# A mixture-of-experts layer whose residual rows come from the expert gathers in place of gathers of their own

## The chip, the cores and the metric

One core of a Trainium2 chip runs the kernel. The metric is device microseconds of one execution; the kernel before takes 515.84 us (median of 3 runs, 515.18 to 518.26). One further execution was profiled, and every row below is of that one.

## The reference

One encoder layer on 512 tokens of 1024 features, all in float32: a mixing half (differential attention and a bidirectional recurrence), then a mixture of experts with a residual, then a final norm. The change lies in the second half.

```python
    h = rmsnorm(x, norm2_g[l])
    x = x + hierarchical_moe(h, w_grp[l], w_exp[l], w_gate[l], w_up[l], w_down[l])
return rmsnorm(x, final_g)
...
def hierarchical_moe(h, w_grp, w_exp, w_gate, w_up, w_down):
    g_prob = jax.nn.softmax((t @ w_grp).astype(jnp.float32), axis=-1)
    g_top_p, g_idx = lax.top_k(g_prob, 1)
...
    e_top_logit, e_idx = lax.top_k(e_in_grp, TOP_K)
    e_w = jax.nn.softmax(e_top_logit, axis=-1) * g_top_p
    global_idx = g_idx * EXPERTS_PER_GROUP + e_idx
...
    for e in range(N_EXPERTS):
        hid = jax.nn.silu(t @ w_gate[e]) * (t @ w_up[e])
        out = out + comb[:, e:e + 1] * (hid @ w_down[e])
```

There are 4 groups of 8 experts with a hidden width of 256. A token chooses one group and in it two experts, so both experts of a token are in the same group.

## The kernel before

**Order of the work.** Nothing is issued in the order of the source. Each piece of work is a `task` with an engine, a cost, what it reads and writes, and a priority (`pri`, lower first). `Plan.run` (L188) plays all tasks through a model of the engines and so fixes the order of every engine's queue; the numbers that set priorities stand in one table, `PRM` (L349). Where the plan sees PE idle it puts in small matmuls on zeros (L531, fillers), so that PE stays active. A DMA has a planned time to landing (`lat`; 4.0 for a gather, L1112).

**Mixing half, up to some 245 us.** It leaves x, the residual stream, in SBUF as four tiles of 128 tokens. The output projection of the attention adds its results to x on DVE (L851) or, after a pass on ACT, on POOL (L849); the bits of `ap` in the table say which.

**Router.** `tok_pair(u)` (L883) handles tiles 2u and 2u+1. SP writes x to a DRAM copy, `x2d`. PE transposes x (L897) and multiplies by the router's weights (L906: a moving slice of 128 columns, of which 36 count, 32 experts and 4 groups). DVE picks the group and the two experts (`f1`, L924 to L939). A matmul with a triangle of ones ranks the tokens of each expert (L947, L948); `f3` (L958, L959) takes each token's rank. `hot` (L964) makes one-hots E of the rank among an expert's 64 slots, and L984 makes those among 256 places in a group (EG). `f4`, `f5` (L994 to L1005) compute the two weights of a token. POOL multiplies the choice with what is to travel to the slots: the token's number, its place in its group (L976), its weight and its norm factor (L1009), in a tile `ohw` with three columns of 32.

`tables()` (L1013) turns these round with matmuls by the one-hots (`spread`, L1021): `idx`, the token of each slot (bank `b`, four DVE operations L1030 and L1033), and `slot`, three values a slot (bank `b3`, copied by `g7`, L1039): column 0 is the place, 1 the weight, 2 the norm factor. `places` (L1049) gives `gidx`, the token at each place of a group (DVE, L1053 to L1055).

**Experts.** 16 pairs n of experts, two at a time, 64 slots each, so a pair fills 128 partitions. `gather(n)` (L1122): POOL fetches the rows of x of a pair by `idx` from `x2d` (L1114, an indirect DMA of up to 128 x 4 KB) into one of three buffers XG, in turn, so pairs n and n+3 share one; PE transposes them (L1133, 8 matmuls), DVE and ACT copy them out with the norm's gain (L1137, L1143). The three buffers are zeroed once by POOL (L1125). `expert_pair(n)` (L1146): gate and up matmuls (L1154, 32 records in the trace), silu (L1159, ACT) times up (L1161, DVE), two transposes (L1167) and their copy (L1170, ACT), a one-hot `pm` of the places (L1173, DVE), down matmuls (L1181, two halves of 512 columns). The result, scaled by the weight, is split in two float32r parts: ACT writes `yh` (L482), DVE the rest `yl` (L483).

**Residual and sum.** `places_of(g)` (L1192), once for each group of 4 pairs: POOL zeroes two accumulators of 128 places (L1195) and gathers the group's rows of x into them by `gidx`. `combine(n)` (L1199) multiplies `pm` with `yh` and `yl` (L1214), and DVE adds the result to the accumulators (L1217). After a group's fourth pair `final` (L1222) computes the norm (squares L1230 and L1231, the power on POOL L1235, scaling L1237) and POOL scatters the rows to the output (L1243). In the last pair the second half's accumulator is taken into the bank by PE (L1209).

**Weights.** SP issues 6 MB of weights a pair (L1097 gate and up, L1104 down, L1109 the last pair's down) as soon as buffers are free.

Of the kernel before, what the change touches and what calls it, by code (L numbers as in the profile page):

```python
# [117 lines left out]
class Plan:  # L118
# [69 lines left out]
    def run(self):  # L188
# [85 lines left out]
        while left:  # L274
# [81 lines left out]
def kernel(ctx: ExitStack, tc: tile.TileContext, a, info=None):  # L356
# [42 lines left out]
    slot, idx, g2T, wr = fixed(3 * NP), fixed(NP, I32), fixed(KD), fixed(KD * 36 + 92)  # L399
# [425 lines left out]
    def out_unit(ks, t, n):  # L825
# [3 lines left out]
        for g in sorted({k // 2 for k in ks}):  # L829
# [28 lines left out]
    oht, ohw, gtok = buf(NT * 2 * NE, F32R), buf(NT * 6 * NE), buf(NT * NG, F32R)  # L858
# [3 lines left out]
    slotv = slot.t.rearrange("p (a n) -> p a n", a=3)  # L862

    def load_router(pri):
# [18 lines left out]
    def tok_pair(u):  # L883
# [558 lines left out]
```

## Time and profile before

| | |
|---|---|
| runs of before | 515.18, 515.84, 518.26 us |
| profiled execution | 518.9 us; span 517.1 us, mean granted clock 0.988 |
| PE busy | 495.7 us (96% of the span), 3178 matmul records |
| DVE, ACT, POOL busy | 296.9 (57%), 210.2 (41%), 198.2 us (38%) |
| moved by DMA | 130.56 MB |
| queue of POOL's DMAs | 8.40 MB |
| first transposes of the experts (L1133) start | 267.40 us |
| last down matmul (L1181) ends | 504.7 us |
| gathers (L1114) | 24: 16 for pairs, 8 for accumulators |

The profile's times are us from the start of the span. A "bank" is a PSUM bank, `big` and `sml` are SBUF buffers, `fix` a tile that stays. A record's duration on PE holds some overlap with its neighbours, so sums over PE's work are taken from the chain, which counts each stretch once. Idle time of an engine names who released it.

### The profile page before, as it was taken

What the parts mean: (1) busy time and instruction counts of PE and PEld (TensorE: products, weight loads), DVE (VectorE), ACT (ScalarE), POOL (GpSimd) and SP (SyncE); (2) the same over time, 40 slices, a digit from 0 to 9 for tenths busy, and PEclk for the clock granted to TensorE, in tenths of its full rate; (3) what the DMA queues carried; (4) which work ended last, traced back from release to release, by engine and by line L of the source; (5) the groups of instructions that cost most, each with busy time, mean ns of one, the idle gap of its engine ahead of it and who ended that gap; (6) DMA issues with size and microseconds to landing.
All of it is one profiled execution on the core that took longest, in us unless ns stands there. A gap on an engine that the chain in (4) does not pass through costs nothing.

```text
span 517.1 us, 8524 instructions
## 1 busy us (share of the span) xinstructions
PE 495.7 (96%) x3178; PEld 339.0 (66%) x3178; DVE 296.9 (57%) x551; ACT 210.2 (41%) x424; POOL 198.2 (38%) x264
## 2 busy tenths in 40 slices
PE   9898999999999999999889999999999989999992
PEld 9897789978999878888873344444445434444441
DVE  2887665988868699695750243446433642641324
ACT  4563688768345546346113222242222322321112
POOL 4789825685687721227453030006100430210002
PEclk9899999999999999999999999999999989999997
DMA  8583000310252650989967999999999999999930
GB/s 300 141 292 108 1 1 1 117 46 1 82 176 83 176 150 21 357 317 363 371 199 246 372 412 411 409 413 380 381 408 415 412 410 389 343 412 416 405 122 36
DMA packets 47941, 130.56 MB, mean 252 GB/s; under 512 B 10861, under 2 KB 21274, under 8 KB 44058
## 3 DMA queue, kind: packets, MB, share of 16 engines
q1 hardware_dynamic: 43002, 120.91, 62.2%
q0 software_dynamic: 4608, 8.40, 4.7%
q10 hardware_dynamic: 288, 0.69, 0.5%
q8 instruction: 26, 0.43, 0.3%
q14 instruction: 17, 0.14, 0.1%
HBM read 132.07 MB, written 6.29 MB: 268 GB/s over the span
## 4 chain that ended last, share of the span: by engine, by line
PE 69%; POOL 8%; issue 8%; DMA 8%; DVE 4%; ACT 2%; SPq 0%; POOLq 0%; ACTq 0%
PE bank L1154 18%; PE bank L606 15%; PE bank L1181 8%; PE bank L838 7%; PE bank L1214 5%; POOL big L472 3%; PE bank L750 2%; DMA big<-x2d,fix 2%; PE bank L531 2%; PE bank L784 2%; PE bank L1133 2%; DMA big<-in_x_dram 2%; DMA big<-in_w_gate_dram 2%; DMA out_dram<-big,fix 1%; PE bank L772 1%
## 5 line engine op out<-in xcount | busy, mean ns | idle before, releaser
L606 PE MATMUL bank<-big,big 128*128 128x256 f32 (+1 forms) x768 | 119.5, 315 | 1.8 <-DVE big L479 1.8
L1154 PE MATMUL bank<-big,big 128*64 128x512 f32 x512 | 117.2, 596 | 0.0
L606 PEld LDWEIGHTS bank<-big,big 128*128 128x128 f32 x768 | 107.4, 193 | 10.6 <-DVE big L479 2.0
L1154 PEld LDWEIGHTS bank<-big,big 128*64 128x64 f32 x512 | 36.2, 137 | 65.1 <-issue 63.2
L483 DVE SCALAR_TENSOR_TENSOR big<-bank,fix,big 128x512 fp32r<-128x512 f32 (+1 forms) x40 | 27.8, 695 | 73.6 <-ACT big L482 70.2
L1217 DVE TENSOR_TENSOR big<-big,bank 128x512 f32<-128x512 f32 x62 | 39.5, 681 | 50.5 <-PE bank L1214 44.1
L1181 PE MATMUL bank<-big,big 128*64 128x512 f32 x256 | 60.0, 608 | 0.0
L1235 POOL TENSOR_TENSOR sml<-sml,fix 128x1 f32<-128x1 f32 x8 | 4.5, 561 | 139.2 <-DVE sml L1234 139.1
L472 POOL TENSOR_TENSOR big<-big,big 128x1024 fp32r<-128x1024 f32 (+2 forms) x21 | 50.4, 2403 | 15.2 <-ACT big L470 8.1
L482 ACT ACTIVATE big<-bank,fix 128x512 fp32r<-128x512 f32 (+1 forms) x40 | 25.7, 644 | 58.5 <-PE bank L1181 51.8
L838 PE MATMUL bank<-big,big 128*128 128x512 f32 x192 | 47.4, 397 | 0.0
L531 PE MATMUL bank<-fix 128*128 128x128 bf16 x617 | 42.5, 228 | 1.7 <-DVE fix L533 1.0
L531 PEld LDWEIGHTS <-fix 128*128 128x128 bf16 x617 | 38.3, 102 | 8.1 <-issue 7.0
L1181 PEld LDWEIGHTS bank<-big,big 128*64 128x64 f32 x256 | 18.7, 140 | 34.3 <-issue 31.8
L1114 POOL DMA_INDIRECT big<-x2d,fix x24 | 24.8, 1033 | 40.8 <-PE bank L1133 34.3
L838 PEld LDWEIGHTS bank<-big,big 128*128 128x128 f32 x192 | 35.1, 188 | 8.2 <-issue 1.1
L1159 ACT ACTIVATE big<-bank,fix 128x256 f32<-128x256 f32 x16 | 7.6, 474 | 76.8 <-PE bank L1154 72.3
L472 DVE TENSOR_TENSOR big<-big,big 128x1024 fp32r<-128x1024 f32 (+1 forms) x16 | 30.4, 1912 | 10.2 <-PE bank L606 4.7
L1214 PE MATMUL bank<-big,big 128*128 128x512 f32 x128 | 35.4, 411 | 0.0
L470 ACT CAST big<-big 128x1024 fp32r<-128x1024 f32 (+2 forms) x27 | 27.1, 1016 | 16.6 <-PE bank L606 4.9
L1214 PEld LDWEIGHTS bank<-big,big 128*128 128x128 f32 x128 | 22.4, 189 | 15.0 <-issue 11.4
L479 DVE TENSOR_TENSOR big<-bank,big 128x512 fp32r<-128x512 f32 (+1 forms) x40 | 24.3, 629 | 8.1 <-ACT big L478 8.0
(194 smaller groups left out, 680.9 us busy)
## 6 DMA issues: line engine op xcount, KB each, us to landing
big<-in_w_down_dram SPq DMA_DIRECT2D x30, 1024.0 KB
big<-in_w_gate_dram SPq DMA_DIRECT2D x60, 512.0 KB
big<-in_w_up_dram SPq DMA_DIRECT2D x60, 512.0 KB
big<-in_w_in_dram SPq DMA_DIRECT2D x20, 512.0 KB
big<-in_w_out_dram SPq DMA_DIRECT2D x4, 1024.0 KB
big<-in_x_dram SPq DMA_DIRECT2D x4, 512.0 KB
big<-in_w_gate_dram SPq DMA_DIRECT2D x8, 256.0 KB
big<-in_w_up_dram SPq DMA_DIRECT2D x8, 256.0 KB
```

Of the source, the lines that this page charges most:

```text
L470: lambda e: (e.copy if e is nc.scalar else e.tensor_copy)(hi(), src()), r=r, w=[kw[0]], pri=pri, room=room, two=True)
L472: lambda e: e.tensor_tensor(lo(), src(), hi().bitcast(F32), op=OP.subtract), r=r + [kw[0]], w=[kw[1]], pri=pri,
L482: task("ACT", act(n), lambda e: e.activation(hi(), src(), AF.Copy, scale=scale), r=[bnk, *r], w=[w[0]], pri=pri)
L483: task("DVE", dve(n) + 0.06, lambda e: e.scalar_tensor_tensor(lo(), src(), scale, hi().bitcast(F32), op0=OP.mult, op1=OP.subtract), r=[bnk ...
L531: e.matmul(b[:, :P], wz.t, wz.t, start=True, stop=True)
L606: e.matmul(out(b), lhs(x, k), rhs(y, k), start=(k == 0 and j == 0), stop=(k == KD - 1 and j == 2))
L838: e.matmul(b.t, lh[x], w[y], start=(i == 0), stop=(i == last))
L1114: g = task("POOL", 1.1, lambda e: e.indirect_dma_start(out=dst.ap(), out_offset=None, in_=x2d[:, :], in_offset=bass.IndirectOffsetOnAxis(a ...
L1154: e.matmul(bg.t[s * 64:(s + 1) * 64].rearrange("p (j f) -> p j f", j=2), xgT[n].ap(KD, P)[:, k, s * 64:(s + 1) * 64], w, start=(k == 0), s ...
L1181: e.matmul(by.t[s * 64:(s + 1) * 64], hidT[n].ap(2, P)[:, k, s * 64:(s + 1) * 64], EW[2 * n + s][1].ap(2, D)[:, k, m * 512:(m + 1) * 512], ...
L1214: e.matmul(b.t, pm.ap()[:, t * P:(t + 1) * P], y.ap(), start=(i == 0 and not held), stop=(i == 1))
L1217: task("DVE", dve(S), lambda e, b=b, xs=xs: e.tensor_tensor(xs(), xs(), b.t, op=OP.add), r=[b], w=[(z, m)])
```

## The change

1. The accumulators are no longer zeroed and filled by gathers. The first pair of a group copies its combined result into them (ACT or DVE, new line L1216); the other three add as before.
2. The residual is added where the expert's result is: a fourth column of the slot table holds 1 where the expert is a token's first and 0 where it is the second. Per half: ACT z = by * slot 1 (new L1185), DVE z += gathered x * slot 3 (new L1186), ACT yh = z (new L1188), DVE yl = z - yh (new L1189).
3. `ohw` and the slot table have four columns, with a copy (new L979) and a memset on POOL.
4. Router logits: 64 columns in place of 128. One-hots: one tensor_tensor for a pair of tiles in place of four tensor_scalar (new L965). Index: token numbers start at -2S and 2S is added, so an empty slot is out of bounds without a test: two operations in place of four. `places` is planned later.
5. Table: `re`, `re3` (what room the loads of weights must leave), `ap` (14 of the additions to x on POOL and 18 on DVE, before 10 and 22), `sq`, `a2`, `o1`, `ot`, `ws`, `w0`; the XG buffers are zeroed earlier.

```diff
+LW = 64
...
-PRM = dict(rw=11000, ro=3000, re=3000, re2=6000, pad=0.4, seq="Q0 X0 X1 K0 V0 G0 G1 V1 Q1 K1", mo=7, mr=7, ge=-42, lru=57,
+PRM = dict(rw=11000, ro=3000, re=0, re2=6000, pad=0.4, seq="Q0 X0 X1 K0 V0 G0 G1 V1 Q1 K1", mo=7, mr=7, ge=-42, lru=57,
...
-                        e.matmul(lgv()[:, t % 2], xT.ap()[:, k * P:(k + 1) * P], wr.t[:, k * 36:k * 36 + P], start=(k == 0), stop=(k == KD - 1))
+                        e.matmul(lgv()[:, t % 2], xT.ap()[:, k * P:(k + 1) * P], wr.t[:, k * 36:k * 36 + LW], start=(k == 0), stop=(k == KD - 1))
...
-        def hot(e, j):
-            for t in range(2):
-                e.tensor_scalar(E.ap(2, 2, P)[:, t, j].rearrange("p (s c) -> p s c", s=2), iot.t[:, None, 0:64].to_broadcast([P, 2, 64]),
-                                rselv[:, 2 * u + t, j:j + 1], None, op0=OP.is_equal)
...
+        def hot(e):
+            e.tensor_tensor(E.ap(4, 2, 64), iot.t[:, None, None, 0:64].to_broadcast([P, 4, 2, 64]),
+                            rselv[:, two].rearrange("p t j -> p (t j)")[:, :, None, None].to_broadcast([P, 4, 2, 64]), op=OP.is_equal)
...
+        task("POOL", 0.3, lambda e: e.tensor_copy(ohw.ap(NT, 2, 4 * NE)[:, two, 0, 3 * NE:], ohp[:, :, 0].bitcast(F32)),
+             r=[(oh, u)], w=[(ohw, (u, 3))])
...
-                e.tensor_scalar(none.ap()[rows], mine, 0.0, 8192.0, op0=OP.is_equal, op1=OP.mult)
-            for s in range(2):
-                rows, mine = slice(s * 64, s * 64 + 64), b.t[s * 64:s * 64 + 64, s:NE:2]
-                e.scalar_tensor_tensor(idx.t[rows], mine, -1.0, none.ap()[rows], op0=OP.add, op1=OP.add)
+                e.tensor_scalar(idx.t[rows], mine, 2.0 * S, None, op0=OP.add)
...
-        task("PE", 1.0, places, r=[*EGs, gtok], w=[bp], pri=pl.pri + 60)
+        task("PE", 1.0, places, r=[*EGs, gtok], w=[bp], pri=pl.pri + 140)
...
-            task("POOL", 1.0, lambda e: e.memset(xg[n].ap(), 0.0), w=[xg[n]], pri=PRM["xz"], after=[mark["lg"]])
+            task("POOL", 1.0, lambda e: e.memset(xg[n].ap(), 0.0), w=[xg[n]], pri=PRM["xz"], after=[mark["o", 2, 1]])
...
-            yh, yl = ys[n][0][m]
-            evac(by, lambda by=by: by.t, lambda yh=yh: yh.ap(), lambda yl=yl: yl.ap(), S, [yh, yl],
-                 scale=slotv[:, 1, n:n + 1], r=[(slot, 1)])
+            (yh, yl), z, xs = ys[n][0][m], buf(S), lambda m=m: xg[n].ap()[:, m * 512:(m + 1) * 512]
+            task("ACT", act(S), lambda e, by=by, z=z: e.activation(z.ap(), by.t, AF.Copy, scale=slotv[:, 1, n:n + 1]), r=[by, (slot, 1)], w=[z])
+            task("DVE", dve(S) + 0.06, lambda e, z=z, xs=xs: e.scalar_tensor_tensor(
+                z.ap(), xs(), slotv[:, 3, n:n + 1], z.ap(), op0=OP.mult, op1=OP.add), r=[xg[n], (slot, 1)], w=[z], two=True)
+            task("ACT", act(S, 0), lambda e, z=z, yh=yh: e.copy(yh.ap(), z.ap()), r=[z], w=[yh])
+            task("DVE", dve(S), lambda e, z=z, yh=yh, yl=yl: e.tensor_tensor(yl.ap(), z.ap(), yh.ap().bitcast(F32), op=OP.subtract),
+                 r=[z, yh], w=[yl], two=True)
...
-    def places_of(g):
-        acc[g] = [buf(D) for _ in range(2)]
-        for q in range(2):
-            task("POOL", 1.0, lambda e, q=q: e.memset(acc[g][q].ap(), 0.0), w=[acc[g][q]],
-                 after=[mark["g", 4 * g - 1] if g else mark["q", 1]])
-            rows_in(acc[g][q], pl.view(gidx, gidx.t[:, q * NG + g:q * NG + g + 1]))
...
+        if n % 4 == 0:
+            acc[n // 4] = [buf(D) for _ in range(2)]
...
-                if not held:
+                if n % 4 == 0:
+                    task({"ACT": act(S, 0), "DVE": dve(S)}, lambda e, b=b, xs=xs: (e.copy if e is nc.scalar else e.tensor_copy)(xs(), b.t),
+                         r=[b], w=[(z, m)])
+                elif not held:
...
-        if n % 4 == 0:
-            pl.pri -= 20
-            places_of(n // 4)
-            pl.pri += 20
```

How it moves instructions is shown at three places. Line numbers in rows of the kernel before are its own, those in rows of the changed kernel are new ones: L1012 is the weights' product (before L1009), L977 the places' (L976), L1213 the combine matmul (L1214), L1237 the power (L1235), L1245 the row scatter (L1243), L532 a filler; L1114, L1133, L1154, L1167 and L1181 are the same in both.

First, POOL at the end of the router, before: the last products into `ohw` and the first three gathers (big_3009, 3036 and 3060 are the XG buffers).

```order
L1009 TENSOR_TENSOR big_2973<-fix 128x4x32 [waits Pool_49]
L976 TENSOR_TENSOR big_2973<-fix,sml_3069 128x4x32 [waits DVE_49]
L1009 TENSOR_TENSOR big_2973<-fix 128x4x32 [waits DVE_49]
L1114 DMA big_3009<-x2d,fix 128x1024 [waits DVE_49,Pool_49]
L1114 DMA big_3036<-x2d,fix 128x1024 [waits Pool_49]
L1114 DMA big_3060<-x2d,fix 128x1024 [waits Pool_49]
```

The same place in the changed kernel, where the XG buffers are big_2751, 2761 and 2773:

```order
L1012 TENSOR_TENSOR big_2151<-fix 128x4x32 [waits Pool_49]
L1012 TENSOR_TENSOR big_2151<-fix 128x4x32 [waits DVE_49]
L977 TENSOR_TENSOR big_2151<-fix,sml_3010 128x4x32 [waits DVE_49,Activation_49]
L1114 DMA big_2751<-x2d,fix 128x1024 [waits DMAHW5_49,DMAHW3_49,DMAHW7_49,DMAHW2_49,DVE_49]
L1114 DMA big_2761<-x2d,fix 128x1024
L1114 DMA big_2773<-x2d,fix 128x1024
L1012 TENSOR_TENSOR big_2151<-fix 128x4x32 [waits DVE_49]
```

The second pair's weight product stood ahead of the first gather and now stands behind the third. The next gather into big_2751 (pair 3) now waits for DVE besides PE.

Second, POOL at the end of group 2, before, with pair 15's gather (into big_3009); big_4317 and 4323 are accumulators of group 3.

```order
L1114 DMA big_4317<-x2d,fix 128x1024 [waits DMASW1_49,Pool_49]
L1114 DMA big_4323<-x2d,fix 128x1024 [waits DMASW2_49,Pool_49]
L1235 TENSOR_TENSOR sml_4427<-sml_4427,fix 128x1 [waits DVE_49]
L1114 DMA big_3009<-x2d,fix 128x1024 [waits DMASW4_49]
L1235 TENSOR_TENSOR sml_4431<-sml_4431,fix 128x1 [waits DVE_49]
L1243 DMA out_dram<-big_4463,fix 512x1024 [waits DVE_49]
```

And in the changed kernel, with pair 15's gather into big_2751:

```order
L1237 TENSOR_TENSOR sml_4469<-sml_4469,fix 128x1 [waits DVE_49,Pool_49]
L1237 TENSOR_TENSOR sml_4471<-sml_4471,fix 128x1 [waits DVE_49,Pool_49]
L1245 DMA out_dram<-big_4485,fix 512x1024 [waits DMAHW6_49,DMAHW4_49,DMAHW7_49,DVE_49,Activation_49]
L1114 DMA big_2751<-x2d,fix 128x1024 [waits DMASW0_49,DVE_49,PE_49]
L1245 DMA out_dram<-big_4516,fix 512x1024 [waits DVE_49,Activation_49]
```

The accumulators' gathers are gone. Pair 15's gather stood ahead of both row scatters of group 2, and now stands behind the first of them and waits for DVE and PE.

Third, PE around pair 15's transposes (L1133), before; the L1181 rows are the last ones of pair 12.

```order
L1181 MATMUL bank_66<-big_4429,big_4480 64x512
L1181 MATMUL bank_66<-big_4439,big_4480 64x512
L1133 MATMUL bank_67<-fix,big_3009 128x128 x4
L1133 MATMUL bank_64<-fix,big_3009 128x128 x4
L1214 MATMUL bank_63<-big_4510,big_4476 128x512
L1214 MATMUL bank_63<-big_4511,big_4476 128x512
L1214 MATMUL bank_62<-big_4510,big_4476 128x512
L1214 MATMUL bank_62<-big_4511,big_4476 128x512
L1154 MATMUL bank_69<-big_4467,big_4243 64x512
```

In the changed kernel the eight L1181 rows of pair 12 stand further up, and between them and these transposes are 16 rows of L1154 and 6 of L1213, of which the last stand here:

```order
L1154 MATMUL bank_69<-big_4480,big_4336 64x512
L1154 MATMUL bank_69<-big_4450,big_4336 64x512
L1154 MATMUL bank_69<-big_4480,big_4336 64x512
L1213 MATMUL bank_67<-big_4497,big_4412 128x512
L1213 MATMUL bank_67<-big_4509,big_4412 128x512
L1213 MATMUL bank_66<-big_4511,big_4412 128x512
L1213 MATMUL bank_66<-big_4521,big_4412 128x512
L1133 MATMUL bank_65<-fix,big_2751 128x128 x4
L1133 MATMUL bank_68<-fix,big_2751 128x128 x4
L1167 MATMUL bank_64<-fix,big_4489 128x128 x2
L1213 MATMUL bank_63<-big_4511,big_4412 128x512
L1213 MATMUL bank_63<-big_4521,big_4412 128x512
```

The transposes of pair 15 followed pair 12's down matmuls directly and now come 22 rows later.

## Rows read from the trace of the kernel before

**Rows 1.** Windows: length; PE, PEld, DVE, ACT, POOL busy (instructions); clock, DMA share, GB/s

```profile
300.00:320.00 20.00, 20.00 (x102) 9.74 (x100) 9.29 (x17) 5.16 (x14) 5.53 (x6) 1.00 1.02 411
420.00:425.00 5.00, 5.00 (x17) 1.58 (x18) 1.36 (x2) 0.69 (x1) 0.85 (x1) 0.68 1.03 413
480.00:500.00 20.00, 20.00 (x111) 8.70 (x108) 6.40 (x12) 2.69 (x5) 0.00 (x0) 1.00 0.79 307
```

**Rows 2.** Waits of SP's queue, 300 to 490 us: total, times, longest

```profile
SPq L1097 <- PE bank L1154: 28.4, 11, 4.8
```

**Rows 3.** The chain that ended last: start, duration, what, times

```profile
290.11 1.09 PE bank L1133 x8
...
307.26 3.43 PE bank L1181 x16
310.69 5.15 PE bank L1154 x24
315.85 2.05 PE bank L1214 x8
...
468.46 1.28 PE bank L531 x21
```

**Rows 4.** PE's timeline, the waits: start, duration, work, [idle before, releaser]

```profile
269.80 1.16 PE L1133 MATMUL bank<-fix,big 128*128 128x128 f32 x8 [1.24 <-DMA big<-x2d,fix]
...
419.29 0.84 PE L1133 MATMUL bank<-fix,big 128*128 128x128 f32 x4 [2.58 <-DMA big<-x2d,fix]
420.06 5.17 PE L1181 MATMUL bank<-big,big 128*64 128x512 f32 x16
```

**Rows 5.** PE's groups by line, 267.4 to 504.8 us: count, busy, mean ns

```profile
L531 PE MATMUL bank<-fix 128*128 128x128 bf16 x159 | 10.9, 220 | 0.0
```

**Rows 6.** PE's timeline in the router

```profile
251.82 1.16 PE L906 MATMUL bank<-fix,big 128*128 128x128 f32 x8
...
261.77 1.14 PE L1049 MATMUL bank<-sml,big 128*128 128x4 f32 x8
```

**Rows 7.** DVE's timeline at the second pair's one-hots and the index

```profile
259.91 1.04 DVE L964 TENSOR_SCALAR big<-fix 128x128 fp32r<-128x128 f32 x4
...
262.05 0.37 DVE L1030 TENSOR_SCALAR sml<-bank 64x16 f32<-64x16 f32 x2
262.45 0.37 DVE L1033 SCALAR_TENSOR_TENSOR fix<-bank,sml 64x16 int32<-64x16 f32 x2
```

**Rows 8.** The page's groups by line: busy us, mean ns

```profile
L1217 DVE TENSOR_TENSOR big<-big,bank 128x512 f32<-128x512 f32 x62 | 39.5, 681 | 50.5 <-PE bank L1214 44.1
```

**Rows 9.** POOL's timeline: the last product, gathers, a scatter, pair 13's gather

```profile
261.95 0.44 POOL L1009 TENSOR_TENSOR big<-fix 128x128 f32<-128x128 f32 x1 [1.48 <-DVE fix L1005]
263.73 1.31 POOL L1114 DMA_INDIRECT big<-x2d,fix  x1 [1.34 <-DVE fix L1055]
...
266.67 0.99 POOL L1114 DMA_INDIRECT big<-x2d,fix  x1 [0.30 <-issue]
...
408.15 1.44 POOL L1243 DMA_INDIRECT out_dram<-big,fix  x1 [2.62 <-issue]
...
411.19 1.04 POOL L1114 DMA_INDIRECT big<-x2d,fix  x1 [0.30 <-DMA big<-in_w_down_dram]
```

**Rows 10.** Landing of gathers issued at 265, at 449, at 412 to 425

```profile
DMA to landing us min/median/max: 4.4/4.4/4.4
...
DMA to landing us min/median/max: 8.2/8.2/8.2
...
DMA to landing us min/median/max: 8.4/9.1/9.7
```

**Rows 11.** ACT's and DVE's timeline at the end

```profile
504.86 0.69 ACT L482 ACTIVATE big<-bank,fix 128x512 fp32r<-128x512 f32 x1 [1.03 <-PE bank L1181]
...
508.35 0.59 ACT L1230 ACTIVATE big<-bank 128x512 f32<-128x512 f32 x1
...
505.58 0.75 DVE L483 SCALAR_TENSOR_TENSOR big<-bank,fix,big 128x512 fp32r<-128x512 f32 x1 [0.97 <-ACT big L482]
```

More of the change, by code (lines that the diff above doesn't have):

```diff
@@ L398 @@
     tokid, desc4, tri, ones = fixed(NT), fixed(NG), fixed(P, BF), fixed(P, BF)
-    slot, idx, g2T, wr = fixed(3 * NP), fixed(NP, I32), fixed(KD), fixed(KD * 36 + 92)
+    slot, idx, g2T, wr = fixed(4 * NP), fixed(NP, I32), fixed(KD), fixed(KD * 36 + LW - 36)
     flag, ovj, nov, novb = fixed(1, I32), fixed(3 * NT), fixed(1), fixed(1, BF)
@@ L861 @@
     w12v, rselv = (z.t.rearrange("p (t j) -> p t j", j=2) for z in (w12, rsel))
-    slotv = slot.t.rearrange("p (a n) -> p a n", a=3)
+    slotv = slot.t.rearrange("p (a n) -> p a n", a=4)
     def load_router(pri):
@@ L879, in load_router @@
         task("POOL", 3.0, g, r=[cst], w=[iot, tokid, desc4, ones, tri], pri=pri, after=[mark[2]])
+        task("POOL", 0.4, lambda e: e.memset(ohw.ap(NT, 2, 4 * NE)[:, :, 1, 3 * NE:], 0.0), w=[(ohw, (0, 3)), (ohw, (1, 3))], pri=pri + 30, after=[mark[9]])
     Es, EGs = [], []
@@ L960, in tok_pair @@
         task("DVE", 0.45, f3, r=[(oh, u), rk], w=[rko, (rsel, u)])
-        def hot(e, j):
-            for t in range(2):
-                e.tensor_scalar(E.ap(2, 2, P)[:, t, j].rearrange("p (s c) -> p s c", s=2), iot.t[:, None, 0:64].to_broadcast([P, 2, 64]),
-                                rselv[:, 2 * u + t, j:j + 1], None, op0=OP.is_equal)
-        ends = [task("DVE", 0.42, lambda e, j=j: hot(e, j), r=[(rsel, u), iot], w=[(E, j)]) for j in range(2)]
+        def hot(e):
+            e.tensor_tensor(E.ap(4, 2, 64), iot.t[:, None, None, 0:64].to_broadcast([P, 4, 2, 64]),
+                            rselv[:, two].rearrange("p t j -> p (t j)")[:, :, None, None].to_broadcast([P, 4, 2, 64]), op=OP.is_equal)
+        ends = [task("DVE", 0.68, hot, r=[(rsel, u), iot], w=[E], two=True)]
         pl.pri += 10
@@ L1013, in tables @@
     def tables():
-        b, b3, bp, none, nog, big = bank(), bank(), bank(), buf(NP), buf(2 * NG), buf(1)
+        b, b3, bp, nog, big = bank(), bank(), bank(), buf(2 * NG), buf(1)
         def spread(e, u, dst, val, f32):
@@ L1029, in g @@
                 rows, mine = slice(s * 64, s * 64 + 64), b.t[s * 64:s * 64 + 64, s:NE:2]
-                e.tensor_scalar(none.ap()[rows], mine, 0.0, 8192.0, op0=OP.is_equal, op1=OP.mult)
-            for s in range(2):
-                rows, mine = slice(s * 64, s * 64 + 64), b.t[s * 64:s * 64 + 64, s:NE:2]
-                e.scalar_tensor_tensor(idx.t[rows], mine, -1.0, none.ap()[rows], op0=OP.add, op1=OP.add)
-        task("DVE", 0.5, g, r=[b], w=[idx, none])
+                e.tensor_scalar(idx.t[rows], mine, 2.0 * S, None, op0=OP.add)
+        task("DVE", 0.37, g, r=[b], w=[idx])
         for u in range(2):
-            task("PE", 0.9, lambda e, u=u: spread(e, u, b3.t[:, :3 * NE], lambda t, j: ohw.ap(NT, 2, 3 * NE)[:, t, j], True),
-                 r=[Es[u], *((ohw, (u, z)) for z in range(3))], w=[b3], pri=pl.pri + 20)
+            task("PE", 0.9, lambda e, u=u: spread(e, u, b3.t[:, :4 * NE], lambda t, j: ohw.ap(NT, 2, 4 * NE)[:, t, j], True),
+                 r=[Es[u], *((ohw, (u, z)) for z in range(4))], w=[b3], pri=pl.pri + 20)
         def g7(e):
@@ L1041, in g7 @@
                 rows = slice(s * 64, s * 64 + 64)
-                e.tensor_copy(slotv[rows], b3.t[rows, :3 * NE].rearrange("p (q n s) -> p q n s", q=3, s=2)[:, :, :, s])
+                e.tensor_copy(slotv[rows], b3.t[rows, :4 * NE].rearrange("p (q n s) -> p q n s", q=4, s=2)[:, :, :, s])
         mark["g7"] = task("DVE", 0.25, g7, r=[b3], w=[(slot, 1)], pri=pl.pri + 20)
```

26 lines of the change are left out of this document (13 added, 13 removed).

## The prediction

> **What bounds the kernel now.** The page's busy shares (TensorE, PE, far ahead of the others) are means over stages, so I read the windows first. In 300 to 320 us, where the experts run, PE is busy for all of its 20 us and the 16 DMA engines are full too (share 1.02, 411 GB/s) [rows 1]. The two are in balance because SP may not issue a weight load before PE has freed its buffer: between 300 and 490 us SP's queue stands 28.4 us waiting for L1154 alone [rows 2]. The chain then shows PE and nothing else: 16 down matmuls 3.43, 24 gate/up matmuls 5.15, 8 combine matmuls 2.05, 8 transposes 1.09 [rows 3]. So from the first transposes (267.40) to the last down matmul (ends 504.7) each us that PE loses or saves is a us of the kernel, unless weights come later than PE. PE loses there in two ways. It waits for gathered rows: 1.24 at 269.80 and 2.58 at 419.29 [rows 4]. And it runs 159 fillers [rows 5], 21 of them 1.28 us long in the chain, 0.061 each [rows 3]. The change touches both. Ahead of 267.40 the router's chain through DVE and POOL bounds, and behind 504.7 the finishing chain.
>
> **The sum.** It is made against the profiled execution (518.9 us, span 517.1). That execution is 3.1 us above the median of the runs, so the differences are taken from it and applied to 515.84.
>
> **1. Router, up to the first transposes: +0.2.** *Logits.* Eight logits matmuls with 128 columns take 1.16, eight others with 4 columns 1.14 [rows 6]: columns hardly count, and 64 in place of 128 are worth nothing by these rows. By columns alone half of 64 x 1.16 / 8 would go, 4.6, of which 1.8 is ahead of DVE's start; that is the other bound. *Fillers.* In the changed order 16 fillers fewer stand ahead of the second pair's logits: 1.0 earlier. *One-hots.* Four tensor_scalar take 1.04 [rows 7]. No row shows a tensor_tensor of 512 from SBUF, so it is bounded by the row of that size with a PSUM operand, 0.681 [rows 8], and above by the old 1.04; I take 0.68, 0.36 saved. *Index.* Two operations of 0.37 together stand where two pairs of them stood, from 262.05 to 262.82 [rows 7]: 0.4 saved. In all the index is some 1.7 earlier, at 261.1. *Where it goes.* POOL starts the first gather 0.9 behind the index (263.73 - 262.82), and the three gathers take 263.73 to 267.66 = 3.93 [rows 9], so they end at 266.0. The weights product of the second pair (L1012, 0.44 [rows 9]) stood ahead of the gathers and now stands behind them (the order's first piece): 266.4. The spread of the slot table needs it, eight matmuls, 1.14 like the others, and stands ahead of the transposes on PE: 267.6, against 267.40. POOL's queue eats the gain in the index. The fourth slot column adds a copy on POOL, and three memsets leave this stretch; both lie beside DVE's chain, which the gathers wait for.
>
> The Trainium skill speaks against the one-hots' new form. By "VectorE: DVE Perf Modes", section "Mode 2×_2P — use both read ports for one tensor", a tensor_scalar can pass two fp32 elements a cycle and a tensor_tensor can't, as its second operand needs the other port; as an estimate from that, 512 elements cost 0.27 us in the old form and 0.53 in the new, and the sum would be 0.6 worse. The row of 1.04 for four operations, 0.26 each, agrees with neither: what these short ones cost isn't their elements.
>
> **2. The wait at the second pair: -1.2.** Its gather is issued about 1.5 behind the first, at some 263.5, and lands 4.4 later without load [rows 10], at 267.9, ahead of its transposes at 268.7. The 1.24 goes.
>
> **3. Fillers: -5.0.** From the first transposes to the last down matmul the order holds 157 fillers before and 75 after: 82 x 0.061. Work of the next pair stands in their places.
>
> **4. The wait at pair 13: -4.3.** Its gather is issued at 411.19, behind the row scatters of group 1, of which the first starts at 408.15 [rows 9]. PE waits 2.58, and the next 16 down matmuls take 5.17 where others take 3.43, with the granted clock at 0.68 [rows 1, 3, 4]: 2.58 + 1.74. In the new order no scatter stands ahead of gather 13.
>
> **5. A new wait for the gathers: +5.9.** Before, the buffer with pair n-3's rows was free once its transposes were done. Now DVE reads these rows for the residual (L1186), behind that pair's down matmuls and a pass on ACT; only then may POOL gather pair n into it. With E the end of pair n-3's down matmuls: ACT's scaling 0.69, DVE 0.75 [rows 11], with ACT's copy of the first half between them: E+2.0, and 0.2 for POOL. What PE has between E and the transposes of n is, by the new order and [rows 3]: for pair 13 8 transposes 1.09, 24 gate/up 5.15 and 10 combine 2.56, 8.8; for 14 32 gate/up 6.87 and 4 combine 1.03, 7.9; for 15 6.87 and 6 combine 1.54, 8.4 (order's third piece); for the others 10.3 to 13.7. A landing of 4.4 costs nothing. A gather in the loaded stretch took 8.2 [rows 10]. With 8.2 pair 13 waits 2.2 + 8.2 - 8.8 = 1.6, pair 14 2.5, pair 15 2.0 and 1.7 more for a row scatter that now stands ahead of it on POOL (order's second piece; 1.44 and a gap of 0.3 [rows 9]), 3.7; the rest 0.1 at most. The bounds are 0 and 7.8. For 13 and 14 I take 8.2, the nearest row. For 15 I take half, 1.8: its gather falls at some 475 us. In 480 to 500 the DMA engines were busy 0.79 of 20 us, that is until 495.8 [rows 1], and this end comes earlier: 2.1 MB of accumulator rows no longer move (5.1 us at 411 GB/s) and 1.05 MB of weights are issued ahead of the first transposes (2.6). On POOL only row scatters are queued behind a waiting gather, and nobody needs these before the end.
>
> The Trainium skill ("DMA: Bandwidth & Descriptors", section "Anatomy of one DMA — SWDGE (gpsimd) path") gives such a transfer a fixed 2.0 us and its bytes at 436 GB/s; 3.2 us is the estimate for 0.52 MB. By it this step is nothing (rival A). The trace has 4.4 without load and 8.2 under it.
>
> **6. The clock behind the new waits: +1.7.** Behind the wait of 2.58 the granted clock was 0.68 and 1.74 went; behind the one of 1.24 the eight transposes took 1.16, about the 1.09 of the chain [rows 1, 3, 4]. Of the three new waits one is as long as the first: 1.74. Bounds 0 and 3.4 (two of them).
>
> **7. The end: +1.8.** Before, ACT and DVE each touched a half once behind the last down matmul (0.69, 0.75); now each twice, with a copy (0.59 by ACT's nearest pass) and a subtraction (0.68 by [rows 8]) more, and 28 and 20 fillers where 3 and 9 were. From the last down matmul to the end of the last square it was 508.94 - 504.7 = 4.24 [rows 11]; following the new order, where ACT and DVE take turns, it comes to 6.05. In the body the same operations are hidden, as ACT is busy 5.16 and DVE 9.29 of 20 us; so are the eight memsets and eight gathers that POOL no longer has (5.53 of 20) [rows 1].
>
> Sum: 0.2 - 1.2 - 5.0 - 4.3 + 5.9 + 1.7 + 1.8 = **-0.9**, so 514.9 us. Could weights be late instead? Their end at 495.8 moves by 5.1 and 2.6 to 488, while PE's last down matmul is due at some 502: no.
>
> **Rivals.** *A, the gathers land in time.* With the unloaded 4.4, steps 5 and 6 are nothing: -8.5, 507.3 us. For it: while PE waits for rows it frees no buffer, so the weight stream that delays them dries up by itself. Against it: under load no row shows a landing near 4.4. *B, landings get worse, and the kernel slower.* The new order starts each gather just when the down matmuls have freed their weight buffers, so SP's next loads go out with it. Landings of 8.4 to 9.7, median 9.1, are in the trace [rows 10]. At 9.1 pairs 13 to 15 wait 2.5, 3.4 and 4.6, pairs 3, 7, 9 and 11 0.7 to 1.0 each (10.3 to 10.6 of PE's work), 14.2 in all; with 3.4 of clock the sum is +9.1, 524.9 us. Slower by over 1% is decided from a landing of 8.6. Against it: the long landings stood close behind other gathers or scatters, and those are fewer now.
>
> **How the numbers follow.** The forecast's own range has step 5 from 4.1 (pair 15 in time) to 7.8 and step 6 from 0 to 3.4: 511.4 to 518.5, all within 1%, about what a measurement of this kernel can tell from no change. I give it 0.47; rival A, with every landing short enough for a time below 510.7, 0.39; B 0.14. So faster 0.39, same 0.47, slower 0.14. The range goes below A by the 1.8 of the logits, to 505.5, and above the forecast's end to 520, where a landing of 8.4 with 3.4 of clock would put it.
>
> **What would show it.** Step 1: the first transposes at 267 to 268, the index at some 261, the gathers ahead of the last L1012. Steps 2 and 4: no wait at pair 1, none behind scatters at pair 13. Step 3: some 75 fillers in that window. Step 5: PE waiting for gathered rows ahead of the transposes of pairs 13 to 15, with landings near 8; no such wait means A, waits at pairs 3 to 11 too mean B. Step 6: a granted clock below 0.8 behind them. Step 7: some 6 us from the last down matmul to the last square. All of it is wrong if PE waits for weights, or if the first transposes come over 2 us from 267.6.

## The result: slower, by a wait that the forecast priced too low

| | before | changed |
|---|---|---|
| median of the runs | 517.05 us (4 runs, 515.18 to 518.27) | 541.20 us (4 runs, 538.73 to 543.49) |
| ratio | | 1.047, 95% interval 1.041 to 1.053 |
| profiled execution, its span | 518.9, 517.1 us | 538.73, 536.9 us |
| mean granted clock | 0.988 | 0.977 |

The profiled execution of the changed kernel is its fastest; the trace explains 19.8 us of span where the medians differ by 24.2. New line numbers are those of the change's section.

The page of the changed kernel: the three counts that changed most, and the group of the experts' transposes.

```profile
PE 502.5 (94%) x3121; PEld 336.3 (63%) x3121; DVE 309.7 (58%) x560; ACT 235.9 (44%) x472; POOL 192.0 (36%) x254
...
q0 software_dynamic: 3456, 6.30, 3.2%
...
L1133 PE MATMUL bank<-fix,big 128*128 128x128 f32 x128 | 22.0, 319 | 17.3 <-DMA big<-x2d,fix 17.3
```

The work is what the change promised: 2.1 MB less in POOL's queue, fewer fillers. But the transposes stood 17.3 us waiting for gathered rows, where it was 4.2 before. PE's timeline shows where (start, duration, work, idle before and its releaser):

```profile
268.14 1.97 PE L1133 MATMUL bank<-fix,big 128*128 128x128 f32 x8 [2.85 <-DMA big<-x2d,fix]
...
354.80 0.71 PE L1133 MATMUL bank<-fix,big 128*128 128x128 f32 x4 [1.29 <-DMA big<-x2d,fix]
...
382.93 1.16 PE L1133 MATMUL bank<-fix,big 128*128 128x128 f32 x8 [1.29 <-DMA big<-x2d,fix]
...
443.25 1.50 PE L1133 MATMUL bank<-fix,big 128*128 128x128 f32 x8 [4.34 <-DMA big<-x2d,fix]
...
445.54 4.52 PE L1181 MATMUL bank<-big,big 128*64 128x512 f32 x16
...
460.36 1.49 PE L1133 MATMUL bank<-fix,big 128*128 128x128 f32 x8 [2.31 <-DMA big<-x2d,fix]
...
482.49 1.97 PE L1133 MATMUL bank<-fix,big 128*128 128x128 f32 x8 [4.92 <-DMA big<-x2d,fix]
```

These are pairs 0, 7, 9, 13, 14 and 15; pair 11 waits 0.33 more. Behind the long ones PE is slower, too: 16 down matmuls take 4.52, and the transposes 1.97 in place of the 1.16 of [rows 4]. The windows give the reason in their seventh figure, the granted clock (columns as in [rows 1]):

```profile
265.00:270.00 5.00, 2.15 (x11) 1.67 (x9) 1.64 (x7) 0.00 (x0) 0.00 (x0) 0.64 0.97 354
270.00:275.00 5.00, 5.00 (x20) 2.28 (x21) 0.40 (x3) 1.97 (x8) 0.00 (x0) 0.68 0.20 78
...
445.00:450.00 5.00, 5.00 (x20) 1.50 (x20) 1.72 (x3) 1.72 (x6) 0.00 (x0) 0.77 0.31 126
460.00:465.00 5.00, 4.64 (x18) 3.76 (x18) 2.34 (x4) 2.41 (x8) 0.00 (x0) 0.66 1.03 422
480.00:485.00 5.00, 2.51 (x11) 2.51 (x12) 0.69 (x1) 0.50 (x2) 0.00 (x0) 0.65 1.06 373
485.00:490.00 5.00, 5.00 (x34) 3.17 (x35) 0.69 (x1) 0.91 (x4) 0.00 (x0) 0.67 0.94 371
```

The stretches from 265, 460 and 480 hold part of the wait itself. Over the 5 us from the end of each wait the clock is 0.50 at pairs 0 and 15, 0.66 at 13 and 14, and 1.00 at 7 and 9. At 445 to 450 the DMA share is 0.31: while PE waited it freed no weight buffers, and SP issues no load between 437.30 and 450.08, so the weight stream could not run ahead in the meantime.

How a wait comes about is seen at pair 13, whose buffer is freed by pair 10. ACT, DVE and POOL, behind pair 10's down matmuls (which end at 429.8):

```profile
428.12 0.69 ACT L1185 ACTIVATE big<-bank,fix 128x512 f32<-128x512 f32 x1 [3.22 <-PE bank L1181]
428.85 0.75 DVE L1186 SCALAR_TENSOR_TENSOR big<-big,fix,big 128x512 f32<-128x512 f32 x1 [3.85 <-ACT big L1185]
...
430.16 0.68 ACT L1185 ACTIVATE big<-bank,fix 128x512 f32<-128x512 f32 x1
430.47 0.69 DVE L1137 TENSOR_TENSOR big<-bank,fix 128x512 f32<-128x512 f32 x1 [0.88 <-PE bank L1133]
...
431.08 0.68 DVE L1189 TENSOR_TENSOR big<-big,big 128x512 fp32r<-128x512 f32 x1
431.68 0.74 DVE L1186 SCALAR_TENSOR_TENSOR big<-big,fix,big 128x512 f32<-128x512 f32 x1
...
433.20 1.48 POOL L1114 DMA_INDIRECT big<-x2d,fix  x1 [11.56 <-PE bank L1154]
```

The second half is scaled at 430.84, but DVE's queue first has L1137 of the pair after next, which waits for PE's transposes, and the first half's subtraction. The read that frees the buffer ends at 432.42, 2.6 us behind the down matmuls, and POOL starts the gather 0.8 later: 3.4, where the forecast had 2.2. (The profile names L1154 as what released it; but each of the gathers of pairs 3 to 14 starts 0.74 to 0.79 behind the end of DVE's second read, whatever it names, so that read is what they wait for.) Then the landing: of the gathers at 259.72, at 433.20 and at 471.50 (pairs 0, 13 and 15):

```profile
DMA to landing us min/median/max: 8.4/8.4/8.4
...
DMA to landing us min/median/max: 10.0/10.0/10.0
...
DMA to landing us min/median/max: 11.0/11.0/11.0
```

433.20 + 10.0 is the 443.2 at which PE goes on. Pair 0's gather has the landing that only loaded ones had before [rows 10]. SP's timeline shows what moves beside it: four weight loads of 512 KB go out with the first gathers (the run at 511.2 below takes them away).

```profile
259.90 0.33 SPq L1097 DMA_DIRECT2D big<-in_w_gate_dram  x1
260.28 1.38 SPq L1097 DMA_DIRECT2D big<-in_w_up_dram  x1
261.76 0.37 SPq L1097 DMA_DIRECT2D big<-in_w_gate_dram  x1
262.18 0.42 SPq L1097 DMA_DIRECT2D big<-in_w_up_dram  x1
```

In the trace of before SP issues no load between 251.80 and 274.58.

### The profile page after: what moved, and what is told of

Read it like the earlier page. It is cut to its first block, busy times and chain, and to the rows that moved or that the text cites. A ratio compares the mean times of both kernels' runs of the same rounds, so it can differ in the third digit from the quotient of the medians.

```text
span 536.9 us, 8367 instructions
## 1 busy us (share of the span) xinstructions
PE 502.5 (94%) x3121; PEld 336.3 (63%) x3121; DVE 309.7 (58%) x560; ACT 235.9 (44%) x472; POOL 192.0 (36%) x254
## 5 line engine op out<-in xcount | busy, mean ns | idle before, releaser
L1154 PE MATMUL bank<-big,big 128*64 128x512 f32 x512 | 119.2, 603 | 0.0
L607 PEld LDWEIGHTS bank<-big,big 128*128 128x128 f32 x768 | 106.1, 190 | 10.2 <-DVE big L480 1.6
L1114 POOL DMA_INDIRECT big<-x2d,fix x16 | 21.4, 1338 | 153.2 <-DVE big L1186 45.5
L1154 PEld LDWEIGHTS bank<-big,big 128*64 128x64 f32 x512 | 33.9, 138 | 61.1 <-issue 56.0
L1186 DVE SCALAR_TENSOR_TENSOR big<-big,fix,big 128x512 f32<-128x512 f32 x32 | 23.9, 748 | 64.8 <-ACT big L1185 64.8
L1181 PE MATMUL bank<-big,big 128*64 128x512 f32 x256 | 58.9, 602 | 0.0
L839 PE MATMUL bank<-big,big 128*128 128x512 f32 x192 | 48.3, 399 | 0.0
L1185 ACT ACTIVATE big<-bank,fix 128x512 f32<-128x512 f32 x32 | 21.9, 684 | 50.5 <-PE bank L1181 50.5
L532 PE MATMUL bank<-fix 128*128 128x128 bf16 x560 | 39.1, 233 | 1.7 <-DVE fix L534 1.0
L1219 DVE TENSOR_TENSOR big<-big,bank 128x512 f32<-128x512 f32 x46 | 29.6, 682 | 18.8 <-PE bank L1213 18.8
L532 PEld LDWEIGHTS <-fix 128*128 128x128 bf16 x560 | 36.0, 105 | 6.2 <-issue 5.1
L1181 PEld LDWEIGHTS bank<-big,big 128*64 128x64 f32 x256 | 17.9, 139 | 34.9 <-issue 33.9
L1133 PE MATMUL bank<-fix,big 128*128 128x128 f32 x128 | 22.0, 319 | 17.3 <-DMA big<-x2d,fix 17.3
L1213 PE MATMUL bank<-big,big 128*128 128x512 f32 x128 | 37.3, 429 | 0.0
L1133 PEld LDWEIGHTS bank<-fix,big 128*128 128x128 f32 x128 | 17.4, 199 | 29.5 <-DMA big<-x2d,fix 18.6
L1213 PEld LDWEIGHTS bank<-big,big 128*128 128x128 f32 x128 | 23.8, 200 | 16.1 <-issue 6.5
L1143 ACT ACTIVATE big<-bank,fix 128x128 f32<-128x128 f32 x64 | 18.2, 368 | 34.1 <-PE bank L1133 30.7
```

Source lines behind the costliest of these rows:

```text
L532: e.matmul(b[:, :P], wz.t, wz.t, start=True, stop=True)
L607: e.matmul(out(b), lhs(x, k), rhs(y, k), start=(k == 0 and j == 0), stop=(k == KD - 1 and j == 2))
L839: e.matmul(b.t, lh[x], w[y], start=(i == 0), stop=(i == last))
L1133: e.transpose(b.t[:, k * P:(k + 1) * P], xg[n].ap().rearrange("p (j k) -> p j k", k=KD)[:, :, kk * 4 + k], ident)
L1154: e.matmul(bg.t[s * 64:(s + 1) * 64].rearrange("p (j f) -> p j f", j=2), xgT[n].ap(KD, P)[:, k, s * 64:(s + 1) * 64], w, start=(k == 0), s ...
L1181: e.matmul(by.t[s * 64:(s + 1) * 64], hidT[n].ap(2, P)[:, k, s * 64:(s + 1) * 64], EW[2 * n + s][1].ap(2, D)[:, k, m * 512:(m + 1) * 512], ...
```

## Experiments

Each differs from the kernel named by the lines shown. The ratios are to runs of the kernel before made beside it. Theory W: DVE's read of the gathered rows holds their buffer, and the plan, which takes a gather for 4.0 us, leaves too little PE work between. Rivals: O, the added operations and their order cost the time; P, the first gathers do.

**A landing in the plan that is true.**

```diff
-            bounds_check=S - 1, oob_is_err=False), r=[ix, x2o], w=[dst], lat=4.0, **kw)
+            bounds_check=S - 1, oob_is_err=False), r=[ix, x2o], w=[dst], lat=8.5, **kw)
```

> The changed kernel; the plan is told 8.5 us from a gather's issue to its landing in place of 4.0, nothing else. In the new order PE has 12.4 to 15.5 us of matmuls between the down matmuls of pair n-3 and the transposes of pair n, where the changed kernel has 7.9 to 13.8. Theory W (the loss is the wait for gathered rows, because their buffer is held by DVE's read of pair n-3, E + 3.4 us, and the rows then land in 7.6 to 11): waits from the fourth pair on fall from 14.5 us to under 2, with the clock behind them some 17 to 19 us go: 521 to 525 us. Rival O (the loss is the longer period of a pair, 14.3 in place of 13.6 us, in the new order and not the waits): waits go but the time stays above 533. Rival P (the first gathers and their clock): at most 3 us change, since the first three gathers stay as they are.

Measured: 517.0 us, ratio 0.999 (0.998 to 1.001). No transpose waits for rows any more, and in the stretches in which the changed kernel's clock fell it is whole:

```profile
445.00:450.00 5.00, 5.00 (x24) 1.89 (x21) 0.14 (x2) 0.55 (x2) 0.00 (x0) 1.00 1.02 366
...
480.00:485.00 5.00, 5.00 (x49) 2.94 (x47) 0.48 (x1) 0.84 (x2) 0.00 (x0) 1.00 1.03 413
```

24 us went with one number that only moves instructions; the gathers themselves still take 7.1 to 10.2. It is more than I expected (521 to 525): I had left too little for the clock behind the waits, which comes to 8.7 (below).

**A fourth buffer.**

```diff
-fl=0.5, xg=3, xz=150
+fl=0.5, xg=4, xz=150
```

> The changed kernel with four row buffers in place of three: gather n waits for DVE's read of pair n-4, so 12.8 to 21.3 us of PE's work lie between. Theory W: the waits from the fourth pair on go as in the run with the longer landing in the plan, though with 134 fillers between the first transposes and the last down matmul in place of 75 (59 x 0.061 = 3.6 us more): 523 to 529 us. Rival O: above 533. Rival P: 538 to 542.

Measured: 518.0 us, ratio 1.001 (0.999 to 1.003), better than expected. One wait is left, the very first, longer than in the changed kernel (PE's timeline), and behind it the clock is low:

```profile
269.63 3.68 PE L1133 MATMUL bank<-fix,big 128*128 128x128 f32 x16 [4.76 <-DMA big<-x2d,fix]
```

```profile
270.00:275.00 5.00, 5.00 (x22) 3.57 (x22) 1.64 (x3) 2.28 (x8) 0.00 (x0) 0.55 0.08 31
```

So two quite different cures of the buffer's wait bring the same. For the first gathers something else is needed.

**The room that loads must leave.**

```diff
-PRM = dict(rw=11000, ro=3000, re=0, re2=6000,
+PRM = dict(rw=11000, ro=3000, re=3000, re2=6000,
...
-re3=1000,
+re3=2000,
```

> The changed kernel with the two numbers for the room that weight loads must leave set back (re 3000, re3 2000). Rival P (weights issued ahead of the first transposes load the queues, so the first three gathers land in 8.4 to 9.7 us in place of 4.4, PE waits 2.85 and its clock falls to 0.83 in 260 to 280 us): landing back at 4.4, first transposes at some 264 to 265 in place of 268.1, 5 to 7 us less: 534 to 536 us, with the waits at pairs 7 to 15 as they are. Theory W: these stay at 12 to 16 us, so no more than those 7 us go.

Measured: 540.3 us, ratio 1.046 (1.042 to 1.050). A miss: the four loads still go out at 259.5 to 261.5, the first gathers land in 7.9 to 9.7, and waits for rows are 15.7 us. These two numbers are not what puts the loads there.

**The router alone.** The kernel before with 64 columns, the new one-hots and the new index.

> The kernel before with the router's edits alone (64 logits columns, one operation for a pair's one-hots, index in two operations); the accumulators are gathered as before and its table stays. Theory W: no new wait, so 515 to 517 us, the gain in the index being at most 1.7 us. Rival: if the new one-hot operation or the narrower logits cost time themselves, the first transposes come later than 268.5 and the time is above 518.

Measured: 517.1 us, ratio 1.000 (0.998 to 1.002), 0.1 above what was expected. The first gather starts at 259.91 (before: 263.73 [rows 9]) and the transposes at 265.57; the lead is gone by the end.

**No read of the rows.** All operations stay, but the residual is left out.

```diff
-            (yh, yl), z, xs = ys[n][0][m], buf(S), lambda m=m: xg[n].ap()[:, m * 512:(m + 1) * 512]
+            (yh, yl), z, xs = ys[n][0][m], buf(S), lambda m=m: fgb.ap()[:, m * 512:(m + 1) * 512]
...
-                z.ap(), xs(), slotv[:, 3, n:n + 1], z.ap(), op0=OP.mult, op1=OP.add), r=[xg[n], (slot, 1)], w=[z], two=True)
+                z.ap(), xs(), slotv[:, 3, n:n + 1], z.ap(), op0=OP.mult, op1=OP.add), r=[fgb, (slot, 1)], w=[z], two=True)
```

> The changed kernel with every operation of the residual in its place, but DVE's L1186 reads the final norm's gain (a tile that stays) in place of the gathered rows; the residual x is left out of the output. The plan's landing stays 4.0. The gather of pair n again waits only for PE's transposes of pair n-3. Theory W (the read holds the buffer, and that alone makes the wait): waits for gathered rows after the first two pairs under 3 us, 517 to 522 us, although ACT and DVE do all that they do in the changed kernel. Rival O (the added operations on ACT and DVE themselves, and the order that they bring, cost the time): 533 us or more.

Measured: 517.6 us, ratio 1.001 (0.998 to 1.003). What is left of waits for rows (total, times, longest) is at the first two pairs:

```profile
PE bank L1133 <- DMA big<-x2d,fix: 2.9, 2, 2.7
```

This settles W against O: ACT and DVE do all that they do in the changed kernel, with the same 4.0 in the plan, and nothing is lost in the body. What costs is that the operand is the gather's buffer: by the waits, and by the order that the plan makes of it (here a pair's period is the shorter one, below).

**Four buffers, true landings, zeroing at its old place.**

```diff
-fl=0.5, xg=3, xz=150
+fl=0.5, xg=4, xz=150
...
-            bounds_check=S - 1, oob_is_err=False), r=[ix, x2o], w=[dst], lat=4.0, **kw)
+            bounds_check=S - 1, oob_is_err=False), r=[ix, x2o], w=[dst], **{"lat": 8.5, **kw})
...
-            task("POOL", 1.0, lambda e: e.memset(xg[n].ap(), 0.0), w=[xg[n]], pri=PRM["xz"], after=[mark["o", 2, 1]])
-        mark["q", n] = rows_in(xg[n], pl.view(idx, idx.t[:, n:n + 1]), seq=mark.get(("g", n - PRM["ga"])))
+            task("POOL", 1.0, lambda e: e.memset(xg[n].ap(), 0.0), w=[xg[n]], pri=PRM["xz"], after=[mark["lg"]])
+        mark["q", n] = rows_in(xg[n], pl.view(idx, idx.t[:, n:n + 1]), seq=mark.get(("g", n - PRM["ga"])), lat=4.5 if n < 3 else 8.5)
```

> Four row buffers, a landing in the plan of 4.5 us for the first three gathers and 8.5 for the others, and the row buffers zeroed where they were in the kernel before (after the logits), so that they take no SBUF ahead of the router. The plan then puts no weight load between the last ones ahead of the gathers and the transposes. Theory P (in the changed kernel the early row buffers push two to four weight loads to the very time of the first gathers, 259.9 to 262.2 us, and these gathers land in 8.4 to 9.7 in place of 4.4): landing 4.3 to 5, no wait of 4.8 us and no clock of 0.55 as with four buffers alone, the first transposes at 264 to 267: 509 to 513 us against 518 of four buffers alone. If the early landing does not matter: 516 to 519.

Measured: 510.4 us, ratio 0.987 (0.985 to 0.990): 7 us below the kernel before. SP issues no load between 252.58 and 270.30. Of the first four gathers (issued at 260.87 to 265.11) the trace gives the landing of the last alone, 4.1. PE's transposes start 1.8 us earlier than in the kernel before, 4.7 behind the first gather:

```profile
252.58 0.59 SPq L1097 DMA_DIRECT2D big<-in_w_up_dram  x1
270.30 0.33 SPq L1097 DMA_DIRECT2D big<-in_w_gate_dram  x1
```

```profile
DMA to landing us min/median/max: 4.1/4.1/4.1
```

```profile
265.58 1.11 PE L1133 MATMUL bank<-fix,big 128*128 128x128 f32 x8
267.23 1.16 PE L1133 MATMUL bank<-fix,big 128*128 128x128 f32 x8 [0.54 <-DMA big<-x2d,fix]
```

**The same with three buffers** (xg=3, all else as in the last run).

> Three row buffers, the same landings in the plan and the zeroing at its old place; two weight loads (in place of four) still fall beside the first gathers. Theory W keeps pairs 3 to 15 free of waits (gaps of 12.4 to 15.5 us of PE's work); theory P leaves part of the first wait, landing 5 to 8 us. The pair's period stays at 14.3 us (transposes of the next pair right behind the down matmuls, L1167 alone between gate/up matmuls) where four buffers have 13.6. So 512 to 517 us.

Measured: 518.1 us, ratio 1.000 (0.999 to 1.002), just above what was expected. Two loads at 262.15 and 262.52 still go out beside the first gathers, the second pair waits 2.78, and the body keeps the longer period (below).

**The table alone**, in the kernel before.

> The kernel before with the changed kernel's table (re, re3, ap, sq, a2, o1, ot, ws, w0) and nothing else. If the table carries part of the loss, as when more weight loads ahead of the first gathers slow these: above 519 us. If it is neutral as theory W has it: 515 to 519 us.

Measured: 518.0 us, ratio 1.001 (0.998 to 1.003): neutral in time. But two weight loads go out at 260.42 and 260.80, just ahead of the first gathers, where before there were none. The second and third gather still land in 4.6 and 4.5.

**Four buffers zeroed at the old place, the plan's landing left at 4.0.**

> Four row buffers and the zeroing at its old place, with the plan's landing left at 4.0: it differs from the run with four buffers alone (518.0 us) in where the buffers are zeroed, and from the run at 510.4 in the plan's landing. Theory P (the early zeroing is what moves weight loads beside the first gathers): landing of the first gathers 4 to 5, no first wait of 4.8, 509 to 513 us. If the plan's landing is what brought 510.4: 516 to 519.

Measured: 511.2 us, ratio 0.988 (0.985 to 0.991). Against the four buffers alone (518.0) only the zeroing has moved, and with it the loads: none between 253.58 and 270.93. The landings of the first gathers, first in the run with four buffers alone, then here:

```profile
DMA to landing us min/median/max: 7.8/8.5/9.0
```

```profile
DMA to landing us min/median/max: 3.7/4.3/4.5
```

So with four buffers the early zeroing is what put weight loads beside the first gathers. With three it is only a part: with the zeroing at its old place two of the changed kernel's four loads stay (262.15 in the run above, 262.26 in the last run below), and the table alone brings two as well. The plan gives the row buffers their SBUF when they are zeroed; that this space was then missing for weights, so that their loads moved onto the gathers, is my reading of the plan and not shown.

**Accumulators gathered as before**, with the router's edits, four buffers and true landings.

> The kernel before with the router's edits, four row buffers and the landings of 4.5 and 8.5 in the plan: the accumulators are still gathered, the residual is not in the experts. If the residual's new place is worth its removed 2.1 MB and gathers once the buffers are right, this stays behind the run at 510.4: 514 to 517 us. If the buffers and the landing alone are the gain: 509 to 512.

Measured: 515.0 us, ratio 0.996 (0.994 to 0.998). It has the buffers and the landings of the run at 510.4, but not the residual's new place, the table and the copies: these are together worth some 4.5 us once the rows come in time.

**Zeroing at its old place, in the changed kernel alone.**

> The changed kernel with the zeroing at its old place and nothing else. Theory W: the waits at pairs 7 to 15 stay (the gaps are 7.9 to 13.8 us as in the changed kernel), and at most the first wait and the clock behind it go: 532 to 540 us.

Measured: 533.3 us, ratio 1.029 (1.026 to 1.032). Of the loss some 8 us go; waits for rows are still 15.7 us. The time is in the range, but not for the reason given: the first wait is not gone, the second pair now waits 2.97. The profiled execution is the slowest of its four (537.2), so the trace does not show where the 8 us went.

## Why the prediction was wrong

**The sum, as it came out.** The span's 19.8 us split by the traces into +0.7 up to the first transposes (267.40 to 268.14), +17.4 from there to the end of the last down matmul (237.3 to 254.7) and +1.8 in the end chain, less 0.1. In the +17.4, the waits went from 3.8 to 14.5 (+10.7; the 14.5 are the six behind pair 0's). Fillers went from 157 to 75 (-5.0), and the 1.7 of the old wait's clock went. The run with the true landing in the plan tells the other two apart, as it has nearly the same order, no wait and a whole clock: its stretch is 231.7 us (270.80 to 502.51), 226.9 without its 78 fillers. The changed kernel's is 235.6 without waits and fillers, so 8.7 is clock; the kernel before's 222.2 without waits, fillers and its lost clock, so 4.7 is order. 10.7 - 5.0 - 1.7 + 8.7 + 4.7 = 17.4. The clock can be checked directly: in stretches of 1 us, PE's busy time times what the granted clock lacks to 1.00 sums to 8.8, of which 2.5 stand behind pair 0's wait and 6.3 behind the others.

The forecast had -0.9. The 20.7 in between are 8.6 in step 5, 7.0 in step 6, 4.7 for an order that no step had, and 0.5 in step 1.

**Step 5 (the new wait, +5.9) is the step that failed, in its size.** Its mechanism is what the runs showed: take the read away (517.6), give it a fourth buffer (518.0), or leave room for it in the plan (517.0), and the loss is gone. Rival B, to which I gave 0.14, even named the direction and the right pairs, apart from pair 3: 7, 9, 11, 13, 14, 15. Pair 14 came as forecast (2.31 for 2.5). Pair 13 waited 4.34 for 1.6, pair 15 4.92 for 1.8, and pairs 7, 9 and 11 together 2.91 for nothing, as three terms were too small. From the down matmuls' end to the gather it is 3.4 at pairs 7, 9, 11 and 13 (2.6 and 2.8 at 14 and 15), not 2.2, as I followed only the residual's own operations and not what DVE's queue has between them. The landing was 10.0, 7.6 and 11.0 us at pairs 13 to 15 and 7.8 to 8.8 at the others, where I took 8.2 from a single row. And pair 15, for which I took half because the weights would soon end, had the longest wait of all: they had not ended (SP still issues weights at 501.59), since PE's waits hold up the stream too. The Trainium skill's figure ("DMA: Bandwidth & Descriptors", section "Anatomy of one DMA — SWDGE (gpsimd) path"), 3.2 us as an estimate, is nearer to the 4.1 of a gather with no load beside it than to the 7.6 to 11.0 of these; rival A fell with it.

**Step 6 (the clock, +1.7) was too small as well: 8.7.** I priced one wait as before. Here the clock fell to 0.50 at four waits: those of 4.34 and 2.31, with some 3 us at that level behind each, and those of 2.85 and 4.92, where it had fallen before the wait ended, with 5 to 6 us behind each. Pair 0's wait of 2.85 and its clock stood in no step.

**Not in the forecast: the order.** In a run of pairs the changed kernel's period is 14.3 us with PE never idle, before it is 13.6. From one pair's down matmuls to the next's, first the changed kernel, then the kernel before:

```profile
324.69 3.60 PE L1181 MATMUL bank<-big,big 128*64 128x512 f32 x16
328.22 1.16 PE L1133 MATMUL bank<-fix,big 128*128 128x128 f32 x8
329.31 3.65 PE L1154 MATMUL bank<-big,big 128*64 128x512 f32 x16
332.89 2.12 PE L1213 MATMUL bank<-big,big 128*128 128x512 f32 x8
334.94 1.94 PE L1154 MATMUL bank<-big,big 128*64 128x512 f32 x8
336.81 0.51 PE L1167 MATMUL bank<-fix,big 128*128 128x128 f32 x2
337.25 1.94 PE L1154 MATMUL bank<-big,big 128*64 128x512 f32 x8
339.02 3.60 PE L1181 MATMUL bank<-big,big 128*64 128x512 f32 x16
```

```profile
320.71 3.60 PE L1181 MATMUL bank<-big,big 128*64 128x512 f32 x16
324.14 5.32 PE L1154 MATMUL bank<-big,big 128*64 128x512 f32 x24
329.39 2.12 PE L1214 MATMUL bank<-big,big 128*128 128x512 f32 x8
331.36 0.60 PE L1133 MATMUL bank<-fix,big 128*128 128x128 f32 x4
331.79 0.40 PE L1167 MATMUL bank<-fix,big 128*128 128x128 f32 x2
332.03 0.60 PE L1133 MATMUL bank<-fix,big 128*128 128x128 f32 x4
332.56 1.94 PE L1154 MATMUL bank<-big,big 128*64 128x512 f32 x8
334.33 3.60 PE L1181 MATMUL bank<-big,big 128*64 128x512 f32 x16
```

The same matmuls stand in both, but the changed order goes more often from expert matmuls (64 columns of weights) to matmuls with 128 and back. L1167 alone takes 337.25 - 336.81 = 0.44 there and 0.24 between transposes. The runs with four buffers and the one without the read are back at 13.6, with all the residual's operations in place; that it is the changes of kind and not something else in the order was not tried by itself.

**Steps 1 and 2.** The first transposes came at 268.14 for 267.6, by two errors that cancel. The index was ready at 259.41, not 261.1 (eight logits matmuls of 64 columns take 1.00 to 1.06, and the second pair's end at 250.84), so the gathers were issued 2.3 earlier than I had them. But they landed in 8.4, not 4.4: that loads can be pushed beside a transfer by an SBUF buffer that is taken earlier was not in my list, and what pushed them there is shown only in part (above). Pair 0 so had a wait of 2.85 and a clock of 0.50 in the 5 us behind it. The one-hots take 0.684 each, as taken from [rows 8]; the Trainium skill's rule on the two forms ("VectorE: DVE Perf Modes", section "Mode 2×_2P — use both read ports for one tensor") would have had the new form lose; it saved 1.04 - 0.68 = 0.36, as four pieces of 128 had cost 0.26 each.

**Steps 3, 4 and 7 held.** 75 fillers; no wait at pair 13 behind row scatters; and from the last down matmul to the last square 528.89 - 522.83 = 6.06 against the 6.05 foretold:

```profile
519.24 3.65 PE L1181 MATMUL bank<-big,big 128*64 128x512 f32 x16
...
528.30 0.59 ACT L1232 ACTIVATE big<-bank 128x512 f32<-128x512 f32 x1
```

The range ended at 520 because I added the bounds of steps 5 and 6 at one landing only; gathers of the kernel before reach 11.9 in its trace, and with 11 B's own working would have passed 530.

## What to carry to other kernels

A new reader of a transfer's buffer is a new wait for the next transfer: count from the reader's true place in its engine's queue, add the landing of a loaded queue, and compare with the work left in between, pair by pair; where a planner has a landing written in, correct that before anything else is judged. A wait on PE can cost more than its length (17.3 us of waits came with 8.7 of clock here). And a buffer that is claimed earlier can move other transfers: look at what SP issues beside the transfer that everything waits for.

## What was not expected of the hardware

Fifteen of the changed kernel's 16 gathers landed in 7.6 to 11.0 us. The other, issued at 361.72, landed in 4.4; SP issued no load between 353.91 and 363.34. The first four of the run with four buffers and the late zeroing, with no load beside them, landed in 3.7 to 4.5. Loads beside a gather did not always slow it that much: with two of them the first gathers landed in 4.2 to 6.9, as far as the traces give it, in three runs (the table alone, and the late zeroing with three buffers, with either landing in the plan). They took 7.8 to 9.0 in the run with four buffers alone, where the DMA engines were still full from 260 to 262 us (share 0.98, against 0.16 to 0.34 in those three).

Behind four of the changed kernel's waits, 2.31 to 4.92 us long, the granted clock over the next 5 us was 0.50 to 0.66, so most of it was spent at the lower of the two levels, 1.2 GHz; behind the waits of 1.29 it was 1.00. The length of a wait did not settle it by itself: in the run with the zeroing alone moved back, the clock was 0.66 in the 5 us behind a wait of 1.69 (ending at 385.00) and 1.00 behind one of 3.10 (ending at 482.83). The mean of 0.977 over the whole span hides this.
